# Another order of the seven up products, a later relu and square, and another order of an MLP's first loads

## The chip, the cores and the metric

The kernel runs on one core of one Trainium2 chip. A core has five engines with a queue of instructions each: TensorE (PE in the profile, with its weight loads as PEld), VectorE (DVE), ScalarE (ACT), GpSimd (POOL) and SyncE (SP). Here POOL does little but issue the transfers that add onto what already lies at their destination, and SP issues nearly all other transfers. The metric is the device time of one execution in microseconds; less is better.

## The reference, cut to what matters

512 tokens of width 1024 go through two layers, chunked attention in the first and a recurrent block in the second. Each of these is followed by a dense MLP of hidden width 4096, and it is in the two MLPs that the change is made:

```python
def sq_relu_mlp(h, w1, w2):
    z = jax.nn.relu(jnp.einsum('bsd,df->bsf', h, w1))
    return jnp.einsum('bsf,fd->bsd', z * z, w2)

# in reference(), for each layer:
    h = h + sq_relu_mlp(rmsnorm(h, norm_mlp[layer]), mlp_w1[layer], mlp_w2[layer])
```

All of it is float32.

## The kernel before, in words

**Precision.** Each float32 matrix product is made of three matmuls (`mm3`, lines 273 to 276). Every operand is split into a high part, rounded to the matmul's format, and a low part that is the rest; high x high, low x high and high x low are added up in the same PSUM bank. For a weight the high part is a cast on ScalarE (line 178, tile `wh`) and the low part a subtraction on VectorE (line 181, tile `wl`). There are five buffers of each, so a weight can be split at most a few products ahead of TensorE.

**The MLP.** `mlp` (line 667) first makes an eighth of the hidden units in plain products: `up(0, j)` for j from 0 to 7, each with one weight of 512 KB (tile `wr`). Then it goes through four rounds, `round_(p)`. A round has seven *steps* for the second matrix (the "down" weights, tiles `b`) and, for the first three rounds, between them fourteen *pieces* for the next part of the first matrix (the "up" weights, tiles `u`, `us`, `kept`). Seven and twice seven, because each 2 x 2 block product is made with seven multiplications instead of eight, in which some of the operands are sums of blocks.

- **Up pieces.** `group(p, g)` (line 790) is a generator; `rise(n)` in the round takes n pieces from it. A piece is 24 matmuls of 256 columns (tile `m` on TensorE). The seven are named by their right operand: 11, r2, 21, r1, r3, 22, r4, in this order; the weights that belong to them are u11, us2, u12, us1, us3, us4, u22. Piece 11 writes bank b1. `S.copy(b6, b1)` (line 809) copies it, and r2, the very next piece, adds onto the copy. r1 starts a bank b5 of its own. Copies of banks to SBUF are `u` (line 813, of b6) and `v` (line 821, of b5). `out_` (line 797) finishes one quarter of the group's result: for two of the four an addition on VectorE (line 802), then relu and square on ScalarE (lines 804 and 805).
- **Down steps.** A step is 24 matmuls of 512 columns (tiles `x` and `y` on TensorE). Its weights are 11, t1, 22, 21, t2, t3, t4, each in two halves. The left operand is a sum of hidden blocks, split by `split` (lines 839 and 840), formed by `opening` (line 844) and `sums` (line 851). `sums(p + 1, False)` stands between the last two pieces of a round, `sums(p + 1, True)` behind the last.
- **Weights as sums.** t1 is b12 with b11 added onto it by two transfers of GpSimd (`first_sum`, line 120, `b<-b`). us1 is one block loaded by SyncE into one of the two buffers `kept`, onto which GpSimd's transfer from memory adds another (`load_up`, lines 134 and 136). us2 is u11 + us1, added on VectorE (line 161). us3 is u11 with another block added by GpSimd (line 163), us4 is u12 + us2 (line 166).

**The plan.** `plan` is the list of all weights in the order in which TensorE uses them. In a round each line of the loop adds the two halves of a step's weight and then two up weights:

```python
            ups = [("u" + n, 4, (layer, 2 * p + g)) for g in range(2) for n in ("11", "s2", "12", "s1", "s3", "s4", "22")]
            for n, kind in enumerate(("11", "t1", "22", "21", "t2", "t3", "t4")):
                plan.extend((kind, half, (layer, p)) for half in range(2))
                if p < 3:
                    plan.extend(ups[2 * n : 2 * n + 2])
```

`want(n)` hands out the next weights and first calls `fetch` (line 138) until three more are split. `fetch` also issues the loads of the *following* group or round as soon as a buffer is done with: behind us1 the load of the next s1 with its accumulation, behind us3 the next 11, behind us4 the next 12, behind u22 the next 22; behind the second half of t2 the next b12, of t3 the next b11 with `first_sum`, of t4 the next b22 and b21.

**The start of an MLP.** While `up(0, j)` runs, the residual is turned (`turn`, 32 small transfers on SP, `d<-turned`, line 734), and the first loads are issued: b11, b12 and their `first_sum` behind j = 1, b22 and b21 behind j = 3, s1 and 22 of the up weights behind j = 5. The last plain weight, for j = 7, is fetched at the beginning of j = 4, and u11 and u12 with it. The tiles b12 and b22 share their memory with the turned blocks.

**What sets the order.** The program's text gives an order of priority. When it is built, a scheduler puts each engine's queue in order: by that priority among the instructions that it takes to be ready, with its own estimate of how long operations and loads take. It can so put an instruction ahead of others that stand before it in the text, as long as the data allow. Once built, each queue runs in its order, and an instruction that waits holds up those behind it.

PSUM has four banks for the up pieces (tag `mm`) and four others; the copies `u` and `v` take turns in two buffers (tag `nsq`).

Of the kernel before, what the change touches and what calls it, by code (L numbers as in the profile page):

```python
# [10 lines left out]
F32 = mybir.dt.float32  # L11
# [29 lines left out]
def trunk(ctx: ExitStack, tc: tile.TileContext, xT, cols, gfin, win, wqkv, wo, rwin, rga, rgx, rwo, w1, w2, out):  # L41
# [96 lines left out]
    def fetch():  # L138
        i = state["next"]
        state["next"] += 1  # L140
        kind, nk, key = plan[i]
        H = wsp.tile([P, 1024], F32R, name=f"wh{i}", tag="wh")
        L = wsp.tile([P, 1024], F32R, name=f"wl{i}", tag="wl")
        n, half = 1024, nk
        if kind[:5] == "plain":
            n = nk * sum(src.shape[1] for src in key)
            raw = wraw.tile([P, 1024], F32, name=f"wr{i}", tag=f"wr{state['plain'] % 3}")
            state["plain"] += 1
            rv = raw[:, :n].rearrange("p (k c) -> p k c", k=nk)
            c0 = 0  # L150
            for n_, src in enumerate(key):
                w = src.shape[1]
                queue = nc.scalar if i == 0 and n_ else nc.sync
                queue.dma_start(rv[:, :, c0 : c0 + w], rows(src))
                c0 += w
        elif kind[0] == "u":
            nk = 4
            following = (key[0], key[1] + 1)
            if kind == "us2":
                raws["us2"] = wraw.tile([P, 1024], F32, name=f"us2_{key[0]}{key[1]}", tag=f"wr{(state['base'] + 2) % 3}")  # L160
                V.tensor_add(raws["us2"], raws["u11"], raws["us1"])
                raws["us3"] = raws["u11"]
                G.dma_start(four(raws["us3"]), rows(upper[key]["21"]), accum_op=ALU.add)
            if kind == "us4":
                raws["us4"] = raws["u12"]
                V.tensor_add(raws["us4"], raws["us4"], raws["us2"])
            raw = raws[kind]
        else:
            nk = 2
            following = (key[0], key[1] + 1)  # L170
            raw = raws[{"t1": "12", "t2": "22", "t3": "11", "t4": "21"}.get(kind, kind), half]
            if kind == "t2":
                V.tensor_add(raw, raw, raws["12", half])
                G.dma_start(raws["21", half], raw, accum_op=ALU.add)
            if kind == "t3":
                V.tensor_sub(raw, raws["22", half], raw)
        if i:
            S.copy(H[:, :n], raw[:, :n])  # L178
        else:
            start_.append(V.tensor_copy(H[:, :n], raw[:, :n]))  # L180
        low = V.tensor_sub(L[:, :n], raw[:, :n], f(H[:, :n]))  # L181
        if not i:
            start_.append(low)
        if kind == "plain_":
            state["base"] = state["plain"] % 3
            load_up((nk_layer[i], 0), "11")
            load_up((nk_layer[i], 0), "12")
        elif kind == "us1":
            load_up(following, "s1")
        elif kind == "us3":  # L190
            load_up(following, "11")
        elif kind == "us4":
            load_up(following, "12")
        elif kind == "u22":
            load_up(following, "22")
        elif kind == "t2" and half:
            load_down(following, "12")
        elif kind == "t3" and half:
            load_down(following, "11")
            first_sum(following)  # L200
        elif kind == "t4" and half:
            load_down(following, "22")
            load_down(following, "21")
        state["ready"].append((nk, H[:, :n].rearrange("p (k c) -> p k c", k=nk), L[:, :n].rearrange("p (k c) -> p k c", k=nk)))
# [32 lines left out]
    def add_mlp(layer):  # L237
        starts.append(len(plan))
        for j in range(KT):
            plan.append(("plain" if j < KT - 1 else "plain_", KT, [w1[layer][:, j * P : (j + 1) * P]]))  # L240
        nk_layer[len(plan) - 1] = layer
        for n in range(6):
            c0 = (n + 2) * T
            upper[layer, n] = {
                f"{i + 1}{j + 1}": w1[layer][j * T : (j + 1) * T, c0 + i * U : c0 + (i + 1) * U]
                for i in range(2) for j in range(2)
            }
        for p in range(4):
            down[layer, p] = {
                f"{k + 1}{c + 1}": w2[layer][(2 * p + k) * T : (2 * p + k + 1) * T, c * T : (c + 1) * T]  # L250
                for k in range(2) for c in range(2)
            }
            ups = [("u" + n, 4, (layer, 2 * p + g)) for g in range(2) for n in ("11", "s2", "12", "s1", "s3", "s4", "22")]
            for n, kind in enumerate(("11", "t1", "22", "21", "t2", "t3", "t4")):
                plan.extend((kind, half, (layer, p)) for half in range(2))
                if p < 3:
                    plan.extend(ups[2 * n : 2 * n + 2])
# [409 lines left out]
    def mlp(ly, norm):  # L667
        with ExitStack() as mctx:
# [77 lines left out]
            def up(p, j):  # L746
                WH, WL = want(1)
                acc = mmp(f"u{ly}{p}{j}")
                project([acc], [slice(0, P)], WH, WL, xs)
                for h in range(2):  # L750
                    if j % 4 == 0:
                        a[p, j // 4, h] = take(F32, f"a{p}{j // 4}{h}")
                    c = a[p, j // 4, h][:, j % 4]
                    S.activation(c, acc[:, h * U : (h + 1) * U], AF.Relu)
                    S.activation(c, c, AF.Square)
                if j == 0:
                    turn()
                if j == 1:
                    for k in range(KT):
                        scaled(k)  # L760
                    load_down((ly, 0), "11")
                    load_down((ly, 0), "12")
                    first_sum((ly, 0))
                if j == 2:
                    for n in (1, 3, 2, 4):
                        right(n)
                if j == 3:
                    right_split(1)
                    right_split(3)
                    load_down((ly, 0), "22")  # L770
                    load_down((ly, 0), "21")
                if j == 4:
                    right_split(2)
                    opening(0)
                if j == 5:
                    right_split(4)
                    state["kept"] = per.tile([P, 2, 1024], F32, name=f"kept{ly}", tag="hx1")
                    load_up((ly, 0), "s1")
                    load_up((ly, 0), "22")
                if j == 5:  # L780
                    for t in range(4):
                        for c in range(2):
                            squares(t, c)
                if j == 6:
                    V.tensor_add(rq, fs[:, 0:8:2], fs[:, 1:8:2])
                    V.tensor_scalar(rq, rq, 1.0 / D, EPS, ALU.mult, ALU.add)
                    V.reciprocal(rq, rq)
                    V.tensor_scalar(nrq, rq, -1.0, None, ALU.mult)

            def group(p, g):  # L790
# [3 lines left out]
                        for k, (XH, XL) in enumerate(operand(op)):  # L794
                            mm3(bank[:, i * U : (i + 1) * U], WH(k, PAIR[i]), WL(k, PAIR[i]), XH, XL, fresh and k == 0 and i == 0, k == 3, True)

                def out_(i, j, bank, more, sign):
                    if i == j:
                        a[p, g, j] = take(F32, f"a{p}{g}{j}")
                    c = a[p, g, j][:, 2 * i : 2 * i + 2].rearrange("p i c -> p (i c)")  # L800
                    if more is not None:
                        V.tensor_add(c, bank, more)
                        bank = c
                    S.activation(c, bank, AF.Relu, scale=sign)
                    S.activation(c, c, AF.Square)

                b1, b6 = mmp(f"m1{ly}{p}{g}"), mmp(f"m6{ly}{p}{g}")
                piece(b1, "11", True)
                S.copy(b6, b1)  # L809
                yield  # L810
                piece(b6, "r2", False)
                u = wk.tile([P, T], F32, name=f"u{ly}{p}{g}", tag="nsq", bufs=2)
                S.copy(u, b6)
                yield
                piece(b1, "21", False)
                out_(0, 0, b1, None, 1.0)
                yield
                b5 = mmp(f"m5{ly}{p}{g}")
                piece(b5, "r1", True)
                v = wk.tile([P, T], F32, name=f"v{ly}{p}{g}", tag="nsq", bufs=2)  # L820
                S.copy(v, b5)
                yield
                piece(b6, "r3", False)
                out_(1, 1, b6, v, -1.0)
                yield
                piece(b5, "22", False)
                out_(0, 1, b5, u, 1.0)
                yield
                piece(b6, "r4", False)
                out_(1, 0, b6, None, -1.0)  # L830
                yield

# [28 lines left out]
            def round_(p):  # L861
# [59 lines left out]
                rise(2)  # L921
                step("22", X, False, 2, 0)
                rise(1)
                sums(p + 1, False)
                rise(1)
                sums(p + 1, True)

            total = lambda t: fs[:, 2 * t : 2 * t + 1]
# [315 lines left out]
```

## Time and profile before

| | us |
|---|---|
| median of 3 runs | 1075.82 (1073.02 to 1078.41) |
| profiled execution | 1071.08 |
| its span, first to last instruction | 1069.3 |
| PE busy | 1032.4 (97%) |
| DVE busy | 858.5 (80%) |
| ACT busy | 658.5 (62%) |
| POOL busy | 68.1 (6%) |
| mean granted clock of PE | 0.99 |

A row of a list of waits reads: engine and instruction that waited, what ended the wait, then the total in us, how many times, and the longest. A row of a timeline reads: start and length in us, engine, line, operation, the tile written and the tiles read, shapes, how many; in brackets the idle time of the engine before it and what ended that. In the kernel's names `m` is a bank of an up piece, `x` and `y` the banks of the steps, `u` either the plain up products (as a bank of PE) or an up weight.

### The profile page before, as it was taken

Reading aid. Unit: us, or ns where it says so; the run is one execution under the profiler, and the core shown is the slowest. Engines: PE = TensorE matmul, PEld = TensorE weight load, DVE = VectorE, ACT = ScalarE, POOL = GpSimd, SP = SyncE. Lnnn points to the kernel's source line nnn. Section 1 sums busy time; section 2 is a strip of 40 time slices with the busy share of each in tenths; the row PEclk is TensorE's granted clock in tenths of the full one; section 3 lists DMA queues with packets and bytes.
Section 4 is the critical chain, followed back from the end, with each engine's and each line's share of the span. In section 5 each row is a group of like instructions: output and inputs, shape, how many; then the busy total and the mean of one; then the engine's idle time right before and its main releaser. Section 6 shows DMA issues by size and latency. Waiting matters only on the chain.

```text
span 1069.3 us, 14950 instructions
## 1 busy us (share of the span) xinstructions
PE 1032.4 (97%) x5618; PEld 893.5 (84%) x5618; DVE 858.5 (80%) x1216; ACT 658.5 (62%) x1024; POOL 68.1 (6%) x84
## 2 busy tenths in 40 slices
PE   9999999999899989989999999999999989989997
PEld 7888888888689979979988788888789978979986
DVE  7889779867289789579699988986289688589697
ACT  7667567547466556467557686556466566466565
POOL 1000000000101101101000000000101101101000
PEclk9999999999999999999999999999999999999999
DMA  8354253253857837738613413163847837738413
GB/s 277 100 140 132 65 177 99 80 158 84 233 91 184 216 60 197 187 76 211 177 20 99 138 59 94 59 206 101 231 88 189 217 72 185 200 70 203 118 40 99
DMA packets 126248, 145.22 MB, mean 136 GB/s; under 512 B 6240, under 2 KB 98400, under 8 KB 126176
## 3 DMA queue, kind: packets, MB, share of 16 engines
q1 hardware_dynamic: 108320, 114.18, 34.6%
q0 software_dynamic: 17280, 29.36, 16.2%
q8 instruction: 44, 0.72, 0.3%
q10 hardware_dynamic: 576, 0.72, 0.2%
q14 instruction: 28, 0.23, 0.1%
HBM read 116.98 MB, written 2.10 MB: 111 GB/s over the span
## 4 chain that ended last, share of the span: by engine, by line
PE 45%; DVE 13%; DMA 6%; issue 4%; ACT 3%; SPq 1%; DVEq 0%; ACTq 0%; POOLq 0%
PE m L274 6%; PE m L275 6%; PE m L276 6%; DMA kept<-in_w 5%; DVE wl L181 5%; PE y L275 4%; PE y L276 4%; PE y L274 4%; PE x L274 2%; PE x L275 2%; PE x L276 2%; ACT wh L178 2%; PE ro L275 1%; PE ro L274 1%; PE ro L276 1%
## 5 line engine op out<-in xcount | busy, mean ns | idle before, releaser
L181 DVE TENSOR_TENSOR wl<-b,wh 128x1024 fp32r<-128x1024 f32 x112 | 135.8, 1220 | 51.6 <-ACT wh L178 51.5
L178 ACT CAST wh<-b 128x1024 fp32r<-128x1024 f32 x112 | 116.7, 1049 | 83.8 <-PE m L275 46.1
L274 PE MATMUL m<-rH,wh 128*128 128x256 f32 x384 | 110.6, 288 | 14.2 <-ACT m L809 14.2
L276 PE MATMUL m<-rH,wl 128*128 128x256 f32 x384 | 110.0, 287 | 0.0
L275 PE MATMUL m<-rL,wh 128*128 128x256 f32 x384 | 110.0, 287 | 0.0
L178 ACT CAST wh<-wr 128x1024 fp32r<-128x1024 f32 (+1 forms) x73 | 75.1, 1031 | 52.2 <-PE wo L275 11.7
L181 DVE TENSOR_TENSOR wl<-wr,wh 128x1024 fp32r<-128x1024 f32 (+1 forms) x74 | 87.7, 1189 | 23.6 <-ACT wh L178 23.2
L274 PEld LDWEIGHTS m<-rH,wh 128*128 128x128 f32 x384 | 74.8, 195 | 17.5 <-ACT m L809 16.6
L276 PE MATMUL m<-hnH,wl 128*128 128x256 f32 x288 | 81.5, 283 | 0.0
L275 PE MATMUL m<-hnL,wh 128*128 128x256 f32 x288 | 81.5, 283 | 0.0
L274 PE MATMUL m<-hnH,wh 128*128 128x256 f32 x288 | 81.4, 283 | 0.0
L275 PEld LDWEIGHTS m<-rL,wh 128*128 128x128 f32 x384 | 75.0, 195 | 0.9
L276 PEld LDWEIGHTS m<-rH,wl 128*128 128x128 f32 x384 | 75.0, 195 | 0.0
L178 ACT CAST wh<-u 128x1024 fp32r<-128x1024 f32 x48 | 50.3, 1048 | 26.8 <-PE m L275 16.7
L181 DVE TENSOR_TENSOR wl<-u,wh 128x1024 fp32r<-128x1024 f32 x48 | 58.5, 1219 | 3.4 <-ACT wh L178 3.1
L274 PE MATMUL u<-hnH,wh 128*128 128x512 f32 x128 | 51.2, 400 | 7.7 <-ACT wh L178 7.7
L275 PEld LDWEIGHTS m<-hnL,wh 128*128 128x128 f32 x288 | 55.1, 191 | 0.7
L274 PEld LDWEIGHTS m<-hnH,wh 128*128 128x128 f32 x288 | 55.1, 191 | 0.7
L276 PEld LDWEIGHTS m<-hnH,wl 128*128 128x128 f32 x288 | 55.2, 192 | 0.0
L274 PE MATMUL x<-wh,h 128*128 128x512 f32 (+1 forms) x132 | 51.7, 394 | 1.3 <-DVE d L1015 1.3
L275 PE MATMUL y<-wl,hs 128*128 128x512 f32 x128 | 50.5, 395 | 2.2 <-DVE wl L181 2.2
L274 PE MATMUL y<-wh,hs 128*128 128x512 f32 x128 | 50.2, 392 | 1.4 <-DVE d L741 1.4
(373 smaller groups left out, 2963.5 us busy)
## 6 DMA issues: line engine op xcount, KB each, us to landing
b<-in_w SPq DMA_DIRECT2D x64, 512.0 KB, 5.0
b<-b POOLq DMA_DIRECT2D x32, 512.0 KB, 7.8
u<-in_w SPq DMA_DIRECT2D x24, 512.0 KB, 5.2
kept<-in_w SPq DMA_DIRECT2D x24, 512.0 KB, 5.3
wr<-in_wqkv SPq DMA_DIRECT2D x20, 512.0 KB, 4.0
wr<-in_w SPq DMA_DIRECT2D x16, 512.0 KB, 4.2
wr<-in_rwin SPq DMA_DIRECT2D x16, 512.0 KB, 3.6
kept<-in_w POOLq DMA_DIRECT2D x12, 512.0 KB, 6.1
```

Of the source, the lines that this page charges most:

```text
L178: S.copy(H[:, :n], raw[:, :n])
L181: low = V.tensor_sub(L[:, :n], raw[:, :n], f(H[:, :n]))
L274: PE.matmul(acc, WH, XH, start=start, stop=False, skip_group_check=more)
L275: PE.matmul(acc, WH, XL, start=False, stop=False, skip_group_check=more)
L276: PE.matmul(acc, WL, XH, start=False, stop=stop, skip_group_check=more)
```

## The change

No operation is added or taken away. Three things are put in another order.

- **The fifth product second.** The pieces of a group now come as 11, r1, r2, 21, r3, 22, r4, and the plan's up weights as 11, s1, s2, 12, s3, s4, 22. The three banks and both copies' tiles are taken at the group's start. The load of the next s1 is issued behind the fetch of us2 instead of that of us1.
- **Two blocks' relu and square a product later.** `out_` can put off its relu and square; for the second quarter always, and for the third in all groups but those of the last part (p = 3), they stand behind the next piece. For the first two turns of a round `sums(p + 1, False)` stands behind the last piece.
- **First loads in the order of need.** In `up(0, j)` b11 is loaded behind j = 4 instead of 1; behind j = 5 come s1 with its accumulation, then b12 and `first_sum`; behind j = 6 come 22 of the up weights, b22 and b21. In the rounds `first_sum` moves from the second half of t3 to that of t4.

```diff
-        elif kind == "us1":
+        elif kind == "us2":
             load_up(following, "s1")
...
         elif kind == "t3" and half:
             load_down(following, "11")
+        elif kind == "t4" and half:
             first_sum(following)
-        elif kind == "t4" and half:
             load_down(following, "22")
             load_down(following, "21")
...
-            ups = [("u" + n, 4, (layer, 2 * p + g)) for g in range(2) for n in ("11", "s2", "12", "s1", "s3", "s4", "22")]
+            ups = [("u" + n, 4, (layer, 2 * p + g)) for g in range(2) for n in ("11", "s1", "s2", "12", "s3", "s4", "22")]
...
                 if j == 1:
                     for k in range(KT):
                         scaled(k)
-                    load_down((ly, 0), "11")
-                    load_down((ly, 0), "12")
-                    first_sum((ly, 0))
...
                 if j == 3:
                     right_split(1)
                     right_split(3)
-                    load_down((ly, 0), "22")
-                    load_down((ly, 0), "21")
                 if j == 4:
                     right_split(2)
                     opening(0)
+                    load_down((ly, 0), "11")
                 if j == 5:
                     right_split(4)
                     state["kept"] = per.tile([P, 2, 1024], F32, name=f"kept{ly}", tag="hx1")
                     load_up((ly, 0), "s1")
-                    load_up((ly, 0), "22")
+                    load_down((ly, 0), "12")
+                    first_sum((ly, 0))
...
                 if j == 6:
+                    load_up((ly, 0), "22")
+                    load_down((ly, 0), "22")
+                    load_down((ly, 0), "21")
...
-                def out_(i, j, bank, more, sign):
+                later = []
+
+                def out_(i, j, bank, more, sign, hold=False):
...
-                    S.activation(c, bank, AF.Relu, scale=sign)
-                    S.activation(c, c, AF.Square)
-
-                b1, b6 = mmp(f"m1{ly}{p}{g}"), mmp(f"m6{ly}{p}{g}")
+
+                    def finish():
+                        S.activation(c, bank, AF.Relu, scale=sign)
+                        S.activation(c, c, AF.Square)
+
+                    later.append(finish)
+                    if not hold:
+                        held_over()
+
+                def held_over():
+                    while later:
+                        later.pop(0)()
+
+                b1, b5, b6 = (mmp(f"m{n}{ly}{p}{g}") for n in (1, 5, 6))
+                u, v = (wk.tile([P, T], F32, name=f"{n}{ly}{p}{g}", tag="nsq", bufs=2) for n in "uv")
                 piece(b1, "11", True)
                 S.copy(b6, b1)
                 yield
+                piece(b5, "r1", True)
+                S.copy(v, b5)
+                yield
                 piece(b6, "r2", False)
-                u = wk.tile([P, T], F32, name=f"u{ly}{p}{g}", tag="nsq", bufs=2)
                 S.copy(u, b6)
                 yield
                 piece(b1, "21", False)
                 out_(0, 0, b1, None, 1.0)
                 yield
-                b5 = mmp(f"m5{ly}{p}{g}")
-                piece(b5, "r1", True)
-                v = wk.tile([P, T], F32, name=f"v{ly}{p}{g}", tag="nsq", bufs=2)
-                S.copy(v, b5)
-                yield
                 piece(b6, "r3", False)
-                out_(1, 1, b6, v, -1.0)
+                out_(1, 1, b6, v, -1.0, True)
                 yield
                 piece(b5, "22", False)
-                out_(0, 1, b5, u, 1.0)
+                held_over()
+                out_(0, 1, b5, u, 1.0, p < 3)
                 yield
                 piece(b6, "r4", False)
+                held_over()
                 out_(1, 0, b6, None, -1.0)
                 yield
...
                 rise(1)
-                sums(p + 1, False)
+                if p == 2:
+                    sums(p + 1, False)
                 rise(1)
+                if p < 2:
+                    sums(p + 1, False)
                 sums(p + 1, True)
```

## The prediction

> **What bounds the kernel now.** I read the page's first part, then the list of waits for TensorE, then the stretches around each stall.
>
> ```profile
> span 1069.3 us, 14950 instructions
> PE 1032.4 (97%) x5618; PEld 893.5 (84%) x5618; DVE 858.5 (80%) x1216; ACT 658.5 (62%) x1024; POOL 68.1 (6%) x84
> ```
> ```profile
> PE m L274 <- ACT m L809: 14.2, 4, 4.0
> PE u L274 <- ACT wh L178: 7.7, 2, 5.2
> PE y L275 <- DVE wl L181: 2.2, 2, 1.2
> ```
>
> PE is the bound: busy for 97% of the span, and its idle time has few causes. Three of the rows touch this change, 14.2 + 7.7 + 2.2 = 24.1 us. They are six places: the turn from one round to the next, twice in each MLP (four `m` waits), and the start of each MLP (a `u` and a `y` wait each). What is lost there is more than the idle time. In the next rows, one stretch each, stand the busy times of PE, its weight loads, DVE, ACT and POOL, then the granted clock, the share of the DMA engines and GB/s:
>
> ```profile
> 278.00:282.00 4.00, 4.00 (x19) 3.31 (x18) 0.68 (x4) 1.10 (x4) 0.00 (x0) 1.00 1.11 277
> 288.00:292.00 4.00, 4.00 (x12) 2.89 (x13) 4.00 (x4) 2.60 (x3) 0.25 (x1) 0.63 0.78 249
> 389.00:393.00 4.00, 4.00 (x25) 4.00 (x24) 1.07 (x1) 0.07 (x1) 0.00 (x0) 0.62 0.41 120
> 472.00:476.00 4.00, 3.74 (x20) 3.74 (x21) 1.68 (x2) 0.21 (x1) 0.00 (x0) 0.59 0.25 74
> 769.00:773.00 4.00, 3.82 (x10) 2.85 (x11) 3.50 (x3) 4.00 (x8) 0.00 (x0) 0.60 0.85 279
> 869.50:873.50 4.00, 4.00 (x29) 3.81 (x30) 1.42 (x2) 0.97 (x2) 0.00 (x0) 1.00 0.32 93
> 952.00:956.00 4.00, 3.87 (x22) 3.87 (x23) 1.54 (x2) 0.08 (x1) 0.00 (x0) 0.64 0.31 82
> ```
>
> Just ahead of the first stall PE runs at 1.00; in the 4 us behind five of the six it has 0.63, 0.62, 0.59, 0.60 and 0.64. That costs 4 x (0.37 + 0.38 + 0.41 + 0.40 + 0.36) = 7.7 us more. The stall before 869.5 was followed by no dip.
>
> [...]
>
> **The cause at the turns.** On TensorE, VectorE and ScalarE around 388 us (line, operation, tiles, and in brackets the idle time and what ended it):
>
> ```profile
> 382.90 0.28 PE L275 MATMUL m<-hnL,wh 128*128 128x256 f32 x1
> 383.02 0.28 PE L276 MATMUL m<-hnH,wl 128*128 128x256 f32 x1
> 383.14 0.40 PE L274 MATMUL y<-wh,hs 128*128 128x512 f32 x1
> 383.37 0.40 PE L275 MATMUL y<-wl,hs 128*128 128x512 f32 x1
> ...
> 388.65 0.39 PE L274 MATMUL m<-rH,wh 128*128 128x256 f32 x1 [3.74 <-ACT m L809]
> ```
> ```profile
> 337.55 1.23 DVE L181 TENSOR_TENSOR wl<-us,wh 128x1024 fp32r<-128x1024 f32 x1
> ...
> 348.86 1.22 DVE L181 TENSOR_TENSOR wl<-kept,wh 128x1024 fp32r<-128x1024 f32 x1
> ```
> ```profile
> 359.60 0.16 DVE L642 TENSOR_SCALAR sp<-sp 128x8 f32<-128x8 f32 x1
> 365.52 1.23 DVE L161 TENSOR_TENSOR us<-u,kept 128x1024 f32<-128x1024 f32 x1 [5.76 <-DMA kept<-in_w]
> ```
> ```profile
> 384.23 1.05 ACT L839 CAST hs<-s 128x1024 fp32r<-128x1024 f32 x1 [1.59 <-DVE s L854]
> ...
> 388.03 0.57 ACT L809 COPY m<-m 128x512 f32<-128x512 f32 x1
> ```
> ```profile
> 350.11 3.66 DMA kept<-in_w
> 353.84 0.65 issue
> 354.49 11.01 DMA kept<-in_w
> ```
>
> Read from the end. Piece 11 of the new group ends on PE at 383.2, and the next piece, r2, adds onto a copy of its bank (L809). The copy is 0.57 us long, but ScalarE reaches it only at 388.03, behind four casts of about 1.04 us from 384.23 on, the first of which waited for VectorE. VectorE is late because it stood for 5.76 us at L161, the sum for us2, until the accumulating load into `kept` landed. That chain (last fence, of the chain of waits) began at 350.11, when the split of the previous us1 (348.86) had freed `kept`: 3.66 us for the load, 11.01 us for the accumulation.
>
> ```profile
> DVE us L161 <- DMA kept<-in_w: 36.8, 6, 7.4
> ```
>
> This happens six times, at the same six places.
>
> **The change, part by part.** It adds and removes no instruction, byte or transfer; it moves them. From the starts above a 256-column matmul takes 0.12 us and a 512-column one 0.23, so a piece (24 of the first) is 2.9 us and a step (24 of the second) 5.5.
>
> (1) *Piece r1 second.* Behind piece 11 now stands r1, which starts a bank of its own; r2 comes third, behind r1 and a step: the copy of 0.57 us has 2.9 + 5.5 = 8.4 us instead of none. Even today's copy, 388.6 - 383.2 = 5.4 us late, fits. The four `m` waits go: -14.2 us. Bounds: 0, if r1's own weight is as late (rival 3), to -14.2. The copy of b6 to u moves from two pieces and two steps ahead of r3 to one of each; 0.57 us fits into 8.4. Cost 0, or 0.57 if that cover went.
>
> (2) *Earlier load of s1.* us1 is split where us2 is today, and `kept` is free once us2's sum is done as well. Today's us2 was split at 337.55, so the load can go at 338.8 instead of 350.11, 11.3 us sooner; by its own row (3.66 + 0.7 + 11.01) it lands at 354.2, against VectorE's arrival at 359.76. The wait of 5.76 us is covered with 5.5 to spare. us1 itself is wanted by piece r1, at 383.2: landed by 381 with 2.3 us for cast and split, or by 371 if ScalarE's queue takes it ten us ahead. On SP the load passes two loads of b11 (0.88 us of issue); on POOL the accumulation passes the two sums b12 += b11, which are wanted by the step at 383.14. VectorE's wait could become one for the other summand, u11; it had landed when VectorE came, so 0, and at most the 5.76 of today, which (1) hides.
>
> (3) *Relu and square a product later.* They keep ScalarE from standing at a sum that VectorE has not made. The sums of the next round move behind the last piece: 2.9 us later, but y's first step also starts 2.9 us later, since r1 stands ahead of it. Cost 0; -0.5 to +2.9 us a turn if not.
>
> (4) *First loads.* SyncE's queue at the first MLP's start (start, length, transfers), the median from issue to landing of the transfers issued there, and ScalarE at the eighth and last plain weight:
>
> ```profile
> 249.24 20.61 SPq L734 DMA_DIRECT2D d<-turned  x32
> 269.90 2.46 SPq L118 DMA_DIRECT2D b<-in_w  x4
> 272.44 0.50 SPq L154 DMA_DIRECT2D wr<-in_w  x1
> ...
> 281.09 4.75 SPq L134 DMA_DIRECT2D kept<-in_w  x2
> ```
> ```profile
> b<-in_w SPq DMA_DIRECT2D x4, 512.0 KB, 6.0
> b<-b POOLq DMA_DIRECT2D x2, 512.0 KB, 9.7
> wr<-in_w SPq DMA_DIRECT2D x1, 512.0 KB, 14.2
> ```
> ```profile
> 286.70 1.04 ACT L178 CAST wh<-wr 128x1024 fp32r<-128x1024 f32 x1 [2.78 <-DMA wr<-in_w]
> ```
>
> The last plain weight stands behind four loads of b and takes 14.2 us to land; its cast ends at 287.7, and PE has waited the 5.2 us since 282.6 (2.5 us at the second MLP's start). Now the b loads come behind it in the program, so it goes at 269.9 as the first of the batch. The four b took 6.0 us there: landing at 275.9 at most, cast done at 277, 5 us ahead of PE. The `u` waits go: -7.7 us, bounds 0 and -7.7. Next are u11, u12 and s1, whose load (today 281.09) goes some ten us sooner and its accumulation with it, then b12 with its sum. Here is the danger: b12 falls back by four transfers of 0.52 MB, at 277 GB/s (the row 278 to 282) 1.9 us each, 7.6 us. So 269.9 + 7.6 + 6.0 for the load + 9.7 for the sum = 293.2; with 14.2 for the sum, 297.7. PE now wants t1 a plain product and a step (5.5 each) and two pieces after 282.6, at 299.4, less 2.3 for cast and split (1.04 + 1.23): 297. So it fits, with little to spare. I keep the two `y` waits as they are (2.2 us), bounds -2.2 to +4.4.
>
> [...]
>
> (5) *The dips.* Without the five stalls, -7.7 us; bounds 0 and -7.7.
>
> Sum: -14.2 - 7.7 - 7.7 = **-29.6 us**. The profiled execution took 1071.08 us (span 1069.3 and 1.8 around it), which makes 1041.5. The runs' median is 1075.82, 4.7 above it; on that scale I forecast **1046 us**.
>
> **Can the others keep up?**
>
> ```profile
> 311.00:383.00 72.00, 72.00 (x465) 65.84 (x465) 62.18 (x90) 42.93 (x53) 8.73 (x8) 1.00 0.71 175
> ```
>
> Between stalls PE was busy for 72 of 72 us at full clock, with VectorE at 62.2 (86%) and ScalarE at 42.9: both have room.
>
> **Rivals.** *1, the forecast:* 1041 to 1054. *2, half of it:* the loads only change places at a layer's start, t1's sum or s1 is late there instead, and PE stands and dips as today; then only the turns gain, 14.2 + 4 x (0.38 + 0.41 + 0.36) = 18.8 us: 1057; the other half alone (7.7 + 4 x 0.77 = 10.8) gives 1065. For it: the DMA engines are full there (1.11 in the row 278 to 282). Against: the order of need. *3, slower:* us1 is now the second product, not the fourth, and is itself what the accumulation makes; VectorE's 36.8 us at L161 become ScalarE's at the cast of us1, with PE two pieces behind instead of four, and reach PE whole with a dip each: 36.8 + 6 x 1.5 = 45.8 against 31.8 saved at most: +14, 1090. It decides once the accumulation lands after 371 to 381. Against: by part 2 it lands at 354. *4, nothing moves:* the queues are put in order when the program is built, by an estimate of when loads land; L161 was put where `kept` was 5.76 us short of landing. If it is put as far ahead of the earlier landing, VectorE stands as before, and the stalls only change places: 1075.
>
> **How the numbers follow.** Chances: forecast 0.70, half 0.15, nothing 0.07, slower 0.08. What this measurement tells from no change is about 0.5%, 5.4 us. Faster takes the first two, 0.85; same 0.07; slower 0.08. The low end has everything gone (24.1 + 7.7 = 31.8) and 3 us for the spread of the runs: 1041. The high end takes in the half cases, 1065.
>
> **What would show it.** After: no `m` wait at L809; no `u` wait for the last plain weight; L161's wait for `kept` under 10 us of 36.8; clock mean above 0.99. Part 2 is wrong if L161 still waits five us at a turn, part 4 if PE stands at a layer's start for t1 or us1. A PE wait for ScalarE's cast of `kept` would mean rival 3.

## The result and the profile after

The changed kernel takes **1042.25 us** (median of 4 runs, 1041.13 to 1043.22); beside it the kernel before took 1077.06 (4 runs, 1073.02 to 1078.41). The ratio is 0.9683, with a 95% interval from 0.9652 to 0.9713. The profiled execution took 1041.71 us, 29.4 less than the 1071.08 of before.

The page's first part, span and busy times:

```profile
span 1039.9 us, 14946 instructions
PE 1025.5 (99%) x5618; PEld 890.4 (86%) x5618; DVE 863.0 (83%) x1216; ACT 659.3 (63%) x1024; POOL 68.7 (7%) x84
```

PE's busy time fell by 1032.4 - 1025.5 = 6.9 us: the same 5618 matmuls, fewer of them at a low clock (the mean granted clock was 0.990 before and is 0.997). Its idle time fell from 1069.3 - 1032.4 = 36.9 to 1039.9 - 1025.5 = 14.4, by 22.5. Together that is 29.4. The waits of PE and VectorE that stand where the three rows of before stood (who waited, for what, total, times, longest):

```profile
PE y L276 <- DVE ls L852: 1.9, 2, 1.6
PE y L274 <- ACT hs L851: 0.4, 1, 0.4
```
```profile
DVE us L161 <- DMA kept<-in_w: 11.7, 2, 6.6
DVE us L161 <- DMA u<-in_w: 8.7, 4, 3.3
```

No `m` wait and no `u` wait is left. 24.1 us of waits became 2.3: 21.8 of the 22.5. VectorE's six waits for `kept` became two, at the two MLP starts. At the four turns L161 now stands a little while for the other summand, u11.

**A turn.** The first one in the changed kernel, from the timelines of SP, POOL, VectorE, ScalarE and TensorE, and the transfers issued between 334 and 346 us:

```profile
334.67 0.37 SPq L134 DMA_DIRECT2D kept<-in_w  x1
339.10 1.31 POOL L136 DMA_DIRECT2D kept<-in_w  x1 [11.27 <-DMA kept<-in_w]
kept<-in_w POOLq DMA_DIRECT2D x1, 512.0 KB, 6.0
354.90 1.23 DVE L161 TENSOR_TENSOR us<-u,kept 128x1024 f32<-128x1024 f32 x1 [3.28 <-DMA u<-in_w]
379.89 0.58 ACT L822 COPY m<-m 128x512 f32<-128x512 f32 x1
380.01 0.28 PE L274 MATMUL m<-rH,wh 128*128 128x256 f32 x1
387.22 0.28 PE L274 MATMUL m<-rH,wh 128*128 128x256 f32 x1
```

The load of s1 goes at 334.7 and its accumulation at 339.1; that takes 6.0 us, so `kept` has landed by 345.1, almost ten us ahead of L161. Piece 11 ends at 378.85, r1 begins at 380.01, behind five matmuls of the step, and r2 at 387.22. The copy that r2 adds onto is done at 380.5, 6.7 us early.

**The clock.** Four microseconds each behind the start of the first MLP, the first turn, and the start of the second MLP (busy PE, PEld, DVE, ACT, POOL; granted clock; DMA share; GB/s):

```profile
299.50:303.50 4.00, 4.00 (x20) 3.85 (x21) 3.77 (x4) 2.50 (x3) 1.30 (x1) 0.57 0.32 46
378.00:382.00 4.00, 4.00 (x31) 3.79 (x30) 3.43 (x4) 2.47 (x4) 0.00 (x0) 1.00 0.89 131
766.50:770.50 4.00, 4.00 (x29) 3.81 (x30) 3.76 (x4) 2.88 (x4) 1.30 (x1) 1.00 0.24 30
```

One dip is left, behind the `y` wait at the first MLP's start: 4 x 0.43 = 1.7 us.

**The first MLP's start.** ScalarE's timeline there, VectorE's low part of the hidden block (`ls`), PE at step t1 and at r1, and the transfers issued between 268 and 300 us (number, size, median time to landing):

```profile
289.85 1.05 ACT L178 CAST wh<-kept 128x1024 fp32r<-128x1024 f32 x1 [5.56 <-DMA kept<-in_w]
292.41 1.05 ACT L178 CAST wh<-b 128x1024 fp32r<-128x1024 f32 x1 [1.51 <-DMA b<-b]
293.37 0.65 ACT L754 ACTIVATE a<-u 128x256 f32<-128x256 f32 x2
...
295.92 1.05 ACT L851 CAST hs<-a 128x1024 fp32r<-128x1024 f32 x1
...
298.07 1.22 DVE L852 TENSOR_TENSOR ls<-a,hs 128x1024 fp32r<-128x1024 f32 x1
```
```profile
297.02 0.50 PE L274 MATMUL y<-wh,hs 128*128 128x512 f32 x1 [0.40 <-ACT hs L851]
...
299.34 0.55 PE L276 MATMUL y<-wh,ls 128*128 128x512 f32 x1 [1.59 <-DVE ls L852]
...
300.12 0.42 PE L274 MATMUL m<-rH,wh 128*128 128x256 f32 x1
```
```profile
b<-in_w SPq DMA_DIRECT2D x4, 512.0 KB, 9.0
...
b<-b POOLq DMA_DIRECT2D x2, 512.0 KB, 10.6
wr<-in_w SPq DMA_DIRECT2D x1, 512.0 KB, 5.1
```

The last plain weight now lands in 5.1 us (before 14.2). The transfers behind it take longer: b 9.0 (before 6.0), the sums 10.6 (before 9.7). ScalarE stands for `kept` until 289.85 and then for the first half of t1 until 292.41. Behind these two casts stands the relu of the last plain product, whose matmuls had ended at 288.3. So the sums of the hidden blocks, and their split, come late, and step t1 waits for its left operand (`hs`, `ls`), not for its weight. PE asks for that step at 296.6 (297.02 less the 0.40 of waiting), right behind piece 11: in its queue the first four matmuls of t1 stand ahead of r1, which begins only at 300.12.

### The profile page after: what moved, and what is told of

Its sections match the earlier page's. It is cut to its first block, busy times and chain, and to the rows that moved or that the text cites. A ratio compares the mean times of both kernels' runs of the same rounds, so it can differ in the third digit from the quotient of the medians.

```text
span 1039.9 us, 14946 instructions
## 1 busy us (share of the span) xinstructions
PE 1025.5 (99%) x5618; PEld 890.4 (86%) x5618; DVE 863.0 (83%) x1216; ACT 659.3 (63%) x1024; POOL 68.7 (7%) x84
## 4 chain that ended last, share of the span: by engine, by line
PE 82%; DVE 9%; DMA 4%; issue 2%; SPq 2%; ACT 1%; DVEq 0%; POOL 0%; ACTq 0%; POOLq 0%
PE m L276 8%; PE m L275 8%; PE m L274 8%; PE x L274 4%; PE x L275 4%; PE x L276 4%; PE y L276 4%; PE y L274 4%; PE y L275 4%; DVE wl L181 3%; DMA b<-b 2%; PE x L500 2%; PE wo L274 1%; PE wo L275 1%; PE ro L275 1%
## 5 line engine op out<-in xcount | busy, mean ns | idle before, releaser
L178 ACT CAST wh<-wr 128x1024 fp32r<-128x1024 f32 (+1 forms) x73 | 75.0, 1031 | 45.2 <-PE wo L275 11.7
L276 PE MATMUL y<-wh,ls 128*128 128x512 f32 x128 | 50.2, 392 | 1.9 <-DVE ls L852 1.9
L276 PE MATMUL x<-wh,l 128*128 128x512 f32 (+1 forms) x132 | 50.9, 385 | 0.0
```

The costliest lines, as they stand in the source:

```text
L276: PE.matmul(acc, WL, XH, start=False, stop=stop, skip_group_check=more)
```

## The experiments

The theory at the outset was the prediction's: the four `m` waits go because r1 stands between piece 11 and r2. Its rival: VectorE's stand at L161 is the whole cause, and the order of the pieces matters only in so far as it moves that stand. Lines of a variant are shifted by up to four; L161 is L164 in two of them. Every variant computes everything.

**1. The order of the pieces alone**, with the plan and the place of s1's load, and neither the later relu nor the first loads.

```diff
-        elif kind == "us1":
+        elif kind == "us2":
             load_up(following, "s1")
...
-            ups = [... ("11", "s2", "12", "s1", "s3", "s4", "22")]
+            ups = [... ("11", "s1", "s2", "12", "s3", "s4", "22")]
...                 # and r1 second in group()
```

> The kernel before with the new order of pieces and up weights alone (and the load of the next s1 behind us2); relu and square at once, first loads as before. My theory, that the order frees the turns: the m waits of PE at the copy go from 14.2 us to under 1, with three dips of the clock: 18.8 us less than before, 1058. The u waits of 7.7 us stay. Rival, that the order needs the later relu and the first loads: under 9 us less, above 1068.

Measured: 1053.95 us (1051.88 to 1055.41), ratio 0.9806 (0.9775 to 0.9837). PE's and VectorE's waits:

```profile
PE u L274 <- ACT wh L178: 7.6, 2, 5.6
PE y L275 <- DVE wl L181: 2.9, 2, 2.2
```
```profile
DVE us L161 <- DMA u<-in_w: 13.3, 4, 4.4
DVE us L161 <- DMA kept<-in_w: 11.9, 2, 6.4
```

The `m` waits are gone and the two waits at the MLP starts stay. That is the turns' share, and VectorE's waits for `kept` at the turns have gone with them. So this run does not part the theories. It does show that in the new order a stand of up to 4.4 us (for u11, at the turns) does not reach PE.

**2. The first loads alone**, the edits in `up(0, j)` put into the kernel before.

> The kernel before with the new order of an MLP's first loads alone (first_sum in the rounds as before). My theory: the u waits of 7.7 us go with their two dips, 10.8 us less than before, 1066; the m waits stay at 14 us. Rival: the wait only changes place, since in the old order piece r2 adds onto the copy right behind piece 11 and the copy is behind late casts in ScalarE's queue; then a new m wait of 3 to 5 us stands at each MLP's start and the gain is under 4 us, 1073.

Measured: 1066.35 us (10 runs, 1063.43 to 1072.71), ratio 0.9930 (0.9909 to 0.9951).

```profile
PE m L274 <- ACT m L809: 16.6, 6, 4.3
```
```profile
DVE us L161 <- DMA kept<-in_w: 38.9, 6, 8.0
```

The `u` waits are gone; two short `m` waits have come at the MLP starts (0.6 and 1.3 us; six instead of four). The gain in that comparison is 1073.31 - 1066.35 = 7.0 us, and 19.4 for run 1: 26.4 together, where the whole change gained 1074.32 - 1042.22 = 32.1 in a later comparison (run 11). Part of the difference lies at the MLP starts, where the first loads alone leave two `m` waits that the order of the pieces removes; the rest is not traced. The move of `first_sum` in the rounds is in neither of the two runs, and no run tries it alone.

**3. VectorE alone.** The kernel before, with one order more: on VectorE the sum for us2 stands behind the split of the weight fetched just ahead of it, u11. No piece, load or copy is moved in the program.

```diff
-                V.tensor_add(raws["us2"], raws["u11"], raws["us1"])
+                after(V.tensor_add(raws["us2"], raws["u11"], raws["us1"]), state["low"])
...
+        state["low"] = low       # low: the latest weight's split on VectorE
```

> The kernel before with one dependence more, without a wait: on VectorE the sum for us2 (L161) must stand behind the split of the weight before it in the plan, u11. Order, loads and relu as before. My theory, that VectorE standing at L161 ahead of its place is the cause of the late copy: L161 waits under 3 us at the four turns instead of 5 to 7, the m waits fall from 14.2 to under 4 us, some 12 to 18 us less than before, 1059 to 1065. Rival, that the copy right behind its piece is late whatever VectorE does: the m waits stay above 10 us, 1072 or more.

Measured: 1054.13 us (1053.28 to 1054.34), ratio 0.9808 (0.9779 to 0.9837), as fast as run 1 and faster than expected. PE's waits, VectorE's; then at the first turn the accumulation into `kept` (its issue, and the time to landing among the transfers issued between 345 and 370 us) and L161:

```profile
PE u L275 <- ACT wh L178: 4.6, 1, 4.6
PE y L276 <- DVE wl L181: 3.3, 2, 1.9
PE y L275 <- ACT hs L840: 2.5, 1, 2.5
```
```profile
DVE us L161 <- DMA kept<-in_w: 13.6, 2, 7.6
```
```profile
355.50 1.32 POOL L136 DMA_DIRECT2D kept<-in_w  x1 [0.81 <-DMA kept<-in_w]
kept<-in_w POOLq DMA_DIRECT2D x1, 512.0 KB, 10.2
372.23 1.22 DVE L161 TENSOR_TENSOR us<-u,kept 128x1024 f32<-128x1024 f32 x1
```

In the old order, with `kept` landing as late as before (355.5 + 10.2 = 365.7; before 365.5), all four `m` waits are gone. VectorE does other work until 372.2 and then finds both summands there. So the new distance of the copy is not needed for the gain. The old distance was not quite none: in PE's queue seven matmuls of the step stand between piece 11 and r2, 1.7 us (383.87 to 385.53 in this run), and the copy is done at 385.5, just in time.

**4. The load of s1 later in the program**, in the changed kernel.

```diff
-        elif kind == "us2":
+        elif kind == "u12":
             load_up(following, "s1")
```

> The changed kernel with the load of the next s1 issued behind the fetch of u12, which stands where us1 stood before, so as late as before. My theory, that the distance between copy and r2 is enough by itself: VectorE stands at L161 for 4 to 6 us at the turns again, PE does not: no m wait at the copy, time within 2 us of the changed kernel, 1042 to 1044. Rival, that the earlier load carries the gain: m waits of 3 us or waits for the split of us1 at each of four turns, with dips, 1055 to 1060.

Measured: 1041.43 us (1041.12 to 1041.55), ratio 0.9690 (0.9657 to 0.9724). SP's queue at the first turn:

```profile
335.40 0.37 SPq L134 DMA_DIRECT2D kept<-in_w  x1
```

The load went at 335.4 instead of 334.7: the scheduler put it ahead again. The run says nothing on a late load, and run 8 does it with an order on SP.

**5. Relu and square not put off**, and the sums where they were, in the changed kernel.

```diff
-                out_(1, 1, b6, v, -1.0, True)
+                out_(1, 1, b6, v, -1.0)
-                out_(0, 1, b5, u, 1.0, p < 3)
+                out_(0, 1, b5, u, 1.0)
...                 # sums(p + 1, False) between the last two pieces in every round
```

> The changed kernel with relu and square at once in all four quarters and the sums between the last two pieces, as before; order and loads stay changed. My theory: the later relu is worth nothing once VectorE is on time: 1042, within 2 us of the changed kernel. Rival, that it keeps ScalarE free: ScalarE stands at relu for VectorE's addition and PE waits up to 2.9 us at each of the four turns, 1045 to 1054.

Measured: 1041.36 us (1040.67 to 1042.11), ratio 0.9703 (0.9676 to 0.9731). Within what can be measured this part of the change is worth nothing. (The turns at which the changed kernel has the sums behind the last piece are the first two of an MLP, p = 0 and 1.)

**6. The last plain product's relu ahead of t1's cast** on ScalarE, in the changed kernel: the repair for what was seen at the first MLP's start.

```diff
-            S.copy(H[:, :n], raw[:, :n])
+            cast = S.copy(H[:, :n], raw[:, :n])
+            if kind == "t1" and key[1] == 0:
+                after(cast, state["up"])     # the latest square of a plain product
```

> The changed kernel with one order more on ScalarE: at an MLP's start the cast of t1 stands behind the relu and square of the last plain product. The changed kernel still waits 2.3 us in y at an MLP's start for the split of s1. My theory, that the relu was held up behind the cast of t1, which waits for the sum b12 += b11: the y waits for ls and hs go, 1 to 2 us less than the changed kernel, 1040 to 1041. Rival, that t1's own sum is as late: PE waits for wl of t1 instead, the same time, 1042.

Measured: 1037.96 us (1037.45 to 1040.83), ratio 0.9680 (0.9645 to 0.9715); it is timed once more as run 12. ScalarE's timeline and PE's wait:

```profile
290.44 1.05 ACT L178 CAST wh<-kept 128x1024 fp32r<-128x1024 f32 x1 [6.04 <-DMA kept<-in_w]
291.39 0.65 ACT L756 ACTIVATE a<-u 128x256 f32<-128x256 f32 x2
```
```profile
PE y L278 <- DVE ls L854: 0.2, 1, 0.2
```

The relu no longer waits for t1, and 2.1 of the 2.3 us of `y` waits go; PE's busy time falls by 2.0 us (1025.5 to 1023.5), and the dip behind them goes too: the 4 us from 299.5, at 0.57 in the changed kernel, have a clock of 1.00 in run 12.

**7. Run 6 with run 3's order added**, so that VectorE does not stand at the MLP starts either. In the new order the weight fetched just ahead of us2 is the second half of t1.

> As the run with the relu ahead of the cast of t1, and on VectorE the sum for us2 (L161) behind the split of t1's second half, the weight before it in the plan. The changed kernel's VectorE still stands 11.7 + 8.7 us at L161. My theory: those waits go to under 3 us, and PE gains nothing by it, since VectorE has room: 1040 to 1041 as without. Rival, that VectorE's waits still reach PE somewhere: another 2 to 4 us less, 1037.

Measured: 1038.18 us (1037.83 to 1038.48), ratio 0.9674 (0.9646 to 0.9701). L161 no longer waits at all, and PE gains nothing: the 12 us that VectorE stood at the two MLP starts in run 6 cost nothing once run 6's order is there.

**8. A really late load of s1**, in the changed kernel: behind us3's fetch, and on SP behind the load of the next u11.

```diff
-        elif kind == "us2":
-            load_up(following, "s1")
         elif kind == "us3":
-            load_up(following, "11")
+            first = load_up(following, "11")
+            load_up(following, "s1", first)   # after(its SP load, first)
```

> The changed kernel with the load of the next s1 made late for certain: issued behind the fetch of us3 and, on SyncE, tied behind the load of the next 11, so that at the two turns of an MLP it goes at about 349 us of the span instead of 335 and its accumulation lands near 362 instead of 345. (In the run e4_late_s1 the scheduler had put the load where it was before, at 335.) My theory, that the order of the pieces is enough: VectorE stands at L161 for the accumulation, 5 to 8 us at each of the four turns, PE has no m wait at the copy, and the time stays within 2 us of the changed kernel, 1040 to 1044. Rival, that the earlier load carries part of the gain: PE waits 2 to 4 us at each turn for the split of us1 or for the copy, with dips of 1.5 us, 1050 to 1060.

Measured: 1060.60 us (1058.10 to 1061.82), ratio 0.9868 (0.9841 to 0.9896), 18.4 us slower than the changed kernel in the same comparison. The theory in that expectation falls. PE's and VectorE's waits; then at the first turn the load and the accumulation by the chain of waits, VectorE and PE; last the 4 us behind (columns as above):

```profile
PE m L276 <- DVE a L806: 10.0, 4, 5.8
```
```profile
DVE us L164 <- DMA kept<-in_w: 67.7, 12, 11.0
```
```profile
353.88 9.15 DMA kept<-in_w
...
363.73 6.89 DMA kept<-in_w
```
```profile
370.63 1.23 DVE L164 TENSOR_TENSOR us<-u,kept 128x1024 f32<-128x1024 f32 x1 [10.71 <-DMA kept<-in_w]
...
372.91 0.69 DVE L806 TENSOR_TENSOR a<-m,v 128x512 f32<-128x512 f32 x1
```
```profile
373.74 0.55 PE L276 MATMUL m<-rH,wh 128*128 128x256 f32 x1 [5.84 <-DVE a L806]
```
```profile
374.00:378.00 4.00, 4.00 (x20) 4.00 (x21) 2.83 (x4) 3.72 (x5) 0.00 (x0) 0.50 0.43 131
```

The load goes 19.2 us later than in the changed kernel, and the accumulation lands at 370.6. VectorE stands 10.7 us at the sum for us2. Behind that sum in its queue is L806, the sum of the block whose last product was r3; until L806 has read bank b6, piece r4, the second piece behind r3, can't add onto it. PE stands 5.84 us there, and in the 4 us behind it has a clock of 0.50. Of the 16.2 us between the profiled spans of runs 8 and 11 (1056.3 and 1040.1), 10.0 are the waits at L806 and 5.3 more busy time of PE (1029.8 and 1024.5). The copies at which PE stood before have their cover from the new order, and a long stand of VectorE reaches PE through another instruction.

How much of a stand reaches PE differs. The waits at each turn, VectorE's at the sum for us2 and what PE waited in the same stretch (at `m`, and in run 8 also 0.6 us at `y` for `ls` at the last three turns), in us:

| turn | before: VectorE | before: PE | run 8: VectorE | run 8: PE |
|---|---|---|---|---|
| first MLP, first | 5.8 | 3.7 | 10.7 | 5.8 |
| first MLP, second | 7.0 | 3.5 | 9.1 | 1.1 |
| second MLP, first | 6.5 | 3.1 | 11.0 | 3.0 |
| second MLP, second | 7.4 | 4.0 | 8.4 | 0.6 |

So the new order does cover something: stands longer than those of before reach PE with about as much in one turn and with far less in two. It does not cover a stand of any length.

**9. The late load again, with VectorE kept from standing:** run 8 with run 3's order. (The weight fetched just ahead of us2 is t1's second half; the expectation says us1, whose split also stands ahead.)

> The kernel with the late load of s1 (1060.6 us; at the first turn the accumulation into kept lands at 370.6 and VectorE stands 10.7 us at the sum for us2, with the sum of a finished block, L806, and with it the fourth piece r4 behind it), with one order more: on VectorE the sum for us2 stands behind the split of us1, the fetch just ahead of it in the program. The load stays late. If the loss comes from where VectorE stands, and us1 itself is in time (its cast is wanted by about 381), then the m waits behind L806 go: 1040 to 1046. If the late landing itself is the loss (us1, the second product, can't be had earlier), they come back as waits for the cast or the split of kept, and it stays at 1055 to 1062. Between the two, 1046 to 1055, part of each.

Measured: 1042.67 us (1041.05 to 1044.93), ratio 0.9698 (0.9664 to 0.9732). PE's waits, ScalarE's for `kept`, and the first turn on ScalarE and VectorE:

```profile
PE y L279 <- DVE ls L855: 1.6, 1, 1.6
```
```profile
ACT wh L181 <- DMA kept<-in_w: 13.9, 4, 5.7
```
```profile
368.26 1.05 ACT L181 CAST wh<-kept 128x1024 fp32r<-128x1024 f32 x1 [2.92 <-DMA kept<-in_w]
377.56 1.22 DVE L164 TENSOR_TENSOR us<-u,kept 128x1024 f32<-128x1024 f32 x1
```

The landing is nearly as late as in run 8 (at this turn the accumulation is issued at 359.6 and lands at 368.2, in run 8 at 363.7 and 370.6, where VectorE had stood since 359.9), ScalarE even stands 2.92 us for it, and PE does not notice. All of the 18 us come back. So the early landing is not needed either; what sets the time is whether VectorE stands at L161, and for how long, with sums and splits behind it that PE is about to need.

**10. The old order of the pieces with everything else:** the kernel before with run 3's order, the first loads, and run 6's order.

> The kernel before, in its old order of pieces and with relu and square at once, with three other edits: the sum for us2 tied behind the split of u11 on VectorE (as in e3_tie), the first loads of an MLP in the order of need (as in e2_loads), and the relu of the last plain product ahead of the cast of t1 on ScalarE (as in e6_relu). My theory, that late queues and not the distance between the copy and r2 were the cause: no m wait over 1 us at the four turns, and 1037 to 1041. Rival, that the distance is needed: m waits of 1 to 4 us at the MLPs' starts or the turns, 1044 to 1052.

Measured: 1042.26 us (1041.31 to 1045.54), ratio 0.9706 (0.9678 to 0.9734). PE's waits:

```profile
PE m L277 <- ACT m L812: 1.6, 2, 1.0
PE y L279 <- DVE ls L843: 0.5, 1, 0.5
PE y L277 <- ACT hs L842: 0.4, 1, 0.4
```

It has no `m` wait at the turns. It is as fast as the changed kernel without its new order of pieces, and between the two expectations. Against run 12, which has the new order of the pieces (with the places of s1's load and of `first_sum` that go with it and, both worth nothing by runs 5 and 7, the put-off relu and no order on the sum for us2), it is 4.9 us slower. Of these the waits show 2.3 (2.5 less the 0.2 of run 6), all at the MLP starts, where VectorE still stands (5.4 and 5.9 us) and the copy is late. The rest isn't traced to a place.

**11 and 12. The changed kernel and run 6's kernel once more**, in the same comparison as runs 8 and 10.

> The changed kernel itself once more, on the chip of the other runs of this call: 1041 to 1043.

> The kernel of e6_relu once more beside the changed kernel. If the 2.3 us of y waits with their dip are what it saves: 3 to 4 us less than the changed kernel, 1037.5 to 1039. If the difference between the two calls was the chip's: the same as the changed kernel.

Measured: 1042.22 us (1040.82 to 1044.24), ratio 0.9702 (0.9676 to 0.9729), and 1037.39 (1037.19 to 1037.93), ratio 0.9656 (0.9631 to 0.9681). The changed kernel with the relu ahead of t1's cast is the fastest seen, 4.8 us below the changed kernel; the two sets of runs don't overlap.

## Why the prediction was right, step by step

Predicted 1046 (1041 to 1065), measured 1042.25. Against the profiled execution the sum said -29.6 us, and it was -29.4. So close a match is partly luck: the dips gave 0.8 us less than forecast, and 0.7 us of idle time went that is not in its three rows (22.5 against 21.8).

- **(1) The piece order, -14.2: the size right, the reason half wrong.** The four `m` waits are gone and the copy has the 8.4 us that were forecast (378.85 to 387.22). But the step held that this distance is what takes them away. Run 3 shows that the 14.2 go in the old order too, whose cover was 1.7 us and not none, as soon as VectorE doesn't stand. The step also held that today's lateness of VectorE and ScalarE would simply fit. It looked at the copies alone: in run 8 the stand of 10.7 us comes out at r4, through L806, whose cover at that turn was 10.7 - 5.8 = 4.9 us. By that, an estimate, today's 5.76 would have fitted all but 0.9 us. Steps 1 and 2 work on one cause, which the chain in the prediction's first part had named (VectorE at L161); the sum counted it once, and credited the copy. Whether the earlier load alone would have done it in the old order was not run.
- **(2) The earlier load: right in direction, its times pessimistic.** Forecast 338.8 and landed at 354.2; it went at 334.7 and had landed by 345.1. The accumulation took 6.0 us instead of 11.01, which had been taken from the one row of before. L161's wait didn't go to nothing but became one for u11, 8.7 us in four, which the step had named at up to 5.76 each and hidden. The sign to look for, under 10 us for `kept`, was missed narrowly with 11.7: the two MLP starts were left, and run 7 shows them to be free once run 6's order is there.
- **(3) Relu and square later, 0:** run 5 agrees.
- **(4) The first loads, -7.7 for the `u` waits and 2.2 kept:** the `u` waits went, and 2.3 us of `y` waits stayed. That 2.3 is close to the 2.2 kept is luck: the waits of before were for a weight's split, these are for the left operand. The danger was seen in the right place and given the wrong carrier. t1's first half came at 292.4, close to the 293.2 forecast; what was late was not t1 but the relu queued behind t1's cast on ScalarE. The step had not asked what else stands behind a cast that waits. It also had two pieces ahead of t1 in PE's queue, and so wanted it at 299.4; only piece 11 stood there, and PE asked at 296.6. With r1 ahead as well, `ls`, which came at 299.3, would by that reckoning have been in time. Runs 11 and 12 put the price of the late relu at 4.8 us.
- **(5) The dips, -7.7:** PE's busy time fell by 6.9, and the one dip left costs 1.7.
- **The median, +4.7: the term that was mis-sized.** The gap between the profiled execution and the median was carried over, and after the change it was 0.5 us. The granted clock accounts for it, by an estimate: the runs of before range from 1070.44 us at a mean clock of 0.991 to 1079.73 at 0.981, and (0.019 x 1078) - (0.009 x 1070) = 10.9 us of clock lies between them, about as much as the 9.3 us of time. The runs of the changed kernel in the first comparison all had 0.997 and spread over 2.1 us. That it is the dips behind the stalls that vary, and that five of them reduced to one leave less to vary, is the author's estimate; the runs give mean clocks alone.

The rivals. *Half* did not come: the first loads gained 7.0 us by themselves (run 2). In the trace the plain weight takes 9.1 us less to land (5.1 for 14.2) and b 3.0 more (9.0 for 6.0, the median of four); the loads that came later reached PE only through the relu behind t1's cast (part 4). *Slower* was right that a late accumulation is the danger of the new order, and wrong on its way to PE and its price: not ScalarE's cast of us1, which run 9 shows waiting at no cost, but VectorE's queue; 18.4 us when the accumulation lands at 370.6, just short of the 371 to 381 that were to decide. *Nothing moves* did not come, but had the part that decides: it named the place that the scheduler gives L161. In the changed kernel VectorE gets to it at 351.6, 6.5 us behind the landing; in run 8 it is there 10.7 us ahead of it (359.9 against 370.6).

What stays open: why the scheduler puts L161 where it does. That its estimate of a landing is shorter than the landing fits runs 3, 8 and 9 but was not looked at itself.

## What to carry to other kernels

When an engine waits for a copy, follow the lateness back to the first instruction that stood and ask what else is queued behind it: here more distance at the place where the wait showed covered the copy alone, and a stand of VectorE of 10.7 us came out as 5.84 us of PE's at another instruction further down that queue (L806 in run 8). An order on the queue that stood (two lines here, 19 us) tests this before anything is rearranged. And when a load is made to land later or earlier, look again at where the scheduler has put its consumer.

## What the runs showed that was not expected

- The accumulating transfer of 512 KB into `kept` took 11.01 us before and 6.0 after at the first turn; at the MLP start the sums of b took 10.6. The DMA engines' share was 1.08 during the first (354.5 to 365.5) and 0.74 during the second (339.1 to 345.1), which fits a time that depends on what else is under way, but no run tests that; with 6.0 and 11.01 for the same size, one row of such a transfer was a poor term for a sum.
- A load's place in the program did not decide when it went: moved behind u12, it was issued 0.7 us later (run 4).
- The length of a stall did not say whether it brought a dip. The wait of 1.59 us that ended at 299.34 in the changed kernel, with one of 0.40 just ahead of it, was followed by a clock of 0.57 over 4 us (the window of 299.5 above). A stall of before, nearly twice as long, had none (the next 4 us ran at 1.00); its row in the timeline of TensorE:

```profile
869.50 0.38 PE L274 MATMUL m<-rH,wh 128*128 128x256 f32 x1 [3.07 <-ACT m L809]
```
